# Column 1 of a two-level fast matrix product put into the four-product order, and half of column 3's cast copies replaced by direct loads

## The chip, the cores and the metric

One core of a Trainium2 chip runs the kernel. The metric is the device time of one execution in microseconds (us), as a median of several runs. Engines: PE is TensorE, DVE is VectorE, ACT is ScalarE, POOL is GpSimd and SP is SyncE; POOL and SP also issue DMAs, each into a queue of its own.

## What is computed

```python
def setup_inputs():
    m, k, n = 4096, 4096, 4096
    return {
        "a": np.random.randn(m, k).astype(np.float32),
        "b": np.random.randn(k, n).astype(np.float32),
        "bias": np.random.randn(n).astype(np.float32),
    }

def reference(a, b, bias):
    return np.tanh(np.matmul(a, b) + bias)
```

## The kernel before

**Columns and items.** The output is made in four columns of 1024 (numbered 0 to 3 here, so the "second" is column 1 and the "fourth" column 3). Inside a column the unit of work is an item: two blocks of 128 rows, with all of K. Items are numbered n = 0, 1, 2, ... through the whole program: column 0 has 0 to 12, column 1 has 13 to 28, column 2 has 29 to 44, column 3 has 45 to 60. Data are fp16 with fp32 sums in PSUM.

**One level.** An item's a is cut into four transposed quarters a11, a12, a21, a22 and the column's b into b11, b12, b21, b22. Seven products m1 to m7 of sums of these replace eight (`PRODUCTS`, L36): m2 = s2 b11, m5 = s5 b22, m3 = a11 d3, m1 = s1 d1, m4 = a22 d4, m6 = s6 e6, m7 = s7 e7. A whole product is 16 matmuls of 128x512 (`product`, L466). Seven slots (`SLOTS`, L45) make an item; m6 and m7 of an item are run in the slots of the next, and in between DVE reads the PSUM banks and writes them (`after`, L506).

**Two levels.** Where two items that follow each other are taken together, the same product of both (2 x 16 matmuls of 128x512) can be made as seven half products of 8 matmuls of 128x256 each, 56 in all. The left operands then need sums of two items' quarters (made by DVE into tiles `h`), the right operands sums of quarters of b ("forms"). There are two writings of it. `twice` (L663) is used in column 1 only: m3 for the pairs of items (15,16), (17,18), (19,20), (21,22), m4 for the last three of them, m6 for (17,18) and (19,20), whose forms POOL reads back from DRAM one after the other (`pull`, L799). `twice_four` and `four` (L939, L998) are the **four-product order** of columns 2 and 3: a first pair of items has m3 and m4 at two levels while the forms of m2 and m6 are made by DVE and put into DRAM (`put_four`, L761, and `put_sum`, L780, at the slots in `STAGED`, `ASIDE` and `ADDED`); from the next item on `four` runs two items at a time with m2 to m7 without m1 at two levels. m2's and m6's forms are read back by POOL into five buffers (`pull_four`, L828), the others stay in SBUF. The last two items of column 2 have m6 and m7 as whole products ("leaving", `leave` in `four`), while what was overwritten in b is brought back (`BACK`, L95, `give_back`, L986, at steps numbered in `four`).

**Where a comes from.** Items of column 0, and items 24 to 28 of column 1, are "natural": POOL loads fp32 rows of a with a cast to fp16 (`load_nat`, L234) and DVE transposes them (`turn`, L286); SP keeps the quarters and the first sums in DRAM (`keep`). All other items fetch these by SP (`fetch`, L311). Item 23 is the last of column 1 that fetches.

**Where b comes from.** POOL loads a quarter block of fp32 b with a cast (`load_b`, L369, four DMAs a block). For column 3 all 16 blocks are cast during column 1 from DRAM to DRAM (`cast_b`, L365, at the slots in `CAST`, L91), and are read later by one DMA each. Column 3's blocks 0 and 1 are read when column 2 ends, blocks 2 and 3 an item later (`change`).

**Queues.** SP's and POOL's DMAs wait in the order of the program, each for its data, its buffer and for the landing of the DMA eight places ahead in its own queue (the program has eight DMA semaphores a queue and uses them in turn). A DVE instruction waits at the head of DVE's own line in the same way.

Of the kernel before, what the change touches and what calls it, by code (L numbers as in the profile page):

```python
# [59 lines left out]
TWICE = {1: ("m3", "m4"), 2: ("m3", "m4"), 3: ("m3", "m4")}  # L60
# [26 lines left out]
FOURS = {2: 2, 3: 2}  # L87
# [3 lines left out]
CAST = {3: (-106, -103, -100, -97, -94, -91, -88, -85, -82, -79, -76, -73, -70, -67, -64, -61)}  # L91

# [9 lines left out]
PLACE = {  # L102
# [3 lines left out]
}  # L106
OVER = {"e6": (0, 1), "e7": (1, 0)}
# [16 lines left out]
def kernel(  # L124
# [61 lines left out]
    partner, twos, streams, begins, ends_with, firsts = {}, {}, {}, {}, {}, {}  # L186
    for c in TWICE:
        alone = [
            n for n, item in enumerate(items)
            if item[0] == c and item[2] is None and (c > 1 or item[1][0] in early)  # L190
        ]
        alone = alone[: len(alone) // 2 * 2]
        if c in FOURS:
            firsts[alone[0]] = c
            begins[c], ends_with[c] = alone[FOURS[c]], alone[-1] + 1
            alone = alone[: FOURS[c]]
        partner.update(zip(alone[::2], alone[1::2]))
        twos.update({n: [i for i in TWICE[c] if i == "m3" or n > alone[1] or c in FOURS] for n in alone})
        if c in STREAMED:
            streams[c] = alone[2:-2:2]  # L200
            for n in streams[c]:
                twos[n].append("m6")
                twos[n + 1].append("m6")
    second = {v: k for k, v in partner.items()}
    fours = {n for c in FOURS for n in range(begins[c], ends_with[c])}

    plain = max(n for n in partner if items[n][0] == 1) + 2
    guests = {(plain, "a12"), (plain, "a21")}
# [3 lines left out]

    def by_two(n, what):
        return what in twos.get(n, ())
# [96 lines left out]
    def fetch(n, name):  # L311
        for here, there in stored(n, name):
            nc.sync.dma_start(out=here, in_=there)
# [4 lines left out]
    def new_sum(shape, dt, name, n=None):  # L318
        pool = sums
        if n is None or not (by_two(n, "m6") or by_two(n - 2, "m6") or n in fours or items[n][0] in FOURS and (not again(n) or items[n][2] in SPARED) and n < beginning(n)):  # L320
            turns[0] += 1
            pool = spare if turns[0] % 3 == 0 else sums
# [5 lines left out]
    def asum(n, name, half=None):  # L328
# [8 lines left out]
        elif name == "s6" and n in partner and by_two(n, "m6"):  # L337
            s[name] = side[:, :, ds(NB, NB)].rearrange("p a (b m) -> p a b m", m=P)
# [167 lines left out]
    def after(n, s, what, st):  # L506
# [3 lines left out]
        if what == "m2":  # L510
# [3 lines left out]
            if by_two(n, "m4") and n not in firsts:  # L514
# [6 lines left out]
        elif what == "m5":  # L521
            st["c"] = bank(n, s, "c")
            if by_two(n, "m3"):
# [19 lines left out]
        elif what == "m1":  # L543
            if last:
                st["v"] = bank(n, s, "v")
                if n in partner:
                    (twice_four if c in FOURS else twice)(n, "m3", 2)
# [23 lines left out]
        else:  # L571
            if last:
                if n in twos and n + 2 < len(items) and not again(n + 2) and not natural(n + 2) and n + 2 != plain:
                    fetch(n + 2, "a12")
                o = st["ds"] if n + 2 == plain else new_out()
# [46 lines left out]
    def twice_right(what, name):  # L622
        x, y, op = {
            "d1": ((0, 0), (1, 1), SUB), "d4": ((0, 0), (1, 0), ADD), "d3": ((0, 1), (1, 1), ADD),
            "e6": ((0, 0), (0, 1), ADD), "e7": ((1, 0), (1, 1), ADD),
        }[name]
        over = OVER.get(name)
        for i in range(2):
            if (what, name) in rights:
                to = rights[what, name][:, ds(i * TB, TB)]  # L630
            else:
                to = quarter(what, *over, i)
            tt(to, quarter(what, *x, i), quarter(what, *y, i), op)

    def move(what, c, out_, *names):

        for name, (r, j) in (OVER_FOUR if c in FOURS else OVER).items():
# [9 lines left out]
    def twice_left(n, what, name):  # L647
        left = TWO[what][0]
        which = {
            "s2": ((1, 0), (1, 1)), "s5": ((0, 1), (0, 0)), "s1": ((1, 1), (0, 0)),  # L650
            "s6": ((1, 0), (0, 0)), "s7": ((0, 1), (1, 1)),
        }[name]
        x, y = (
            by_four(aset[(n, partner[n])[i]][left])[:, ds(h * TP // TB, TP // TB)] for i, h in which
        )
        tt(by_four(lefts[PLACE[what][name]]), x, y, SUB)

    def twice_clear(n, what):
# [1236 lines left out]
```

## Time and profile before

| what | value |
|---|---|
| time, median of 3 runs (range) | 1516.98 us (1516.84 to 1517.39) |
| the profiled execution: its time, its span | 1514.7 us, 1513.0 us |
| matmuls of 128x512, of 128x256 in the program | 4773, 4312 |
| DMA, mean over the span | 258 GB/s |
| first two-level matmul of columns 1, 2 and 3 | at 458.7, 838.4 and 1204.0 us of the span |

A page of the profile gives each engine's busy time, the span in 40 slices, the DMA queues, the chain that ended last, and groups of like instructions. Other views of the same trace give the waits of an engine, instructions in order of time, and busy times in chosen windows. PEld is the weight load that goes ahead of each matmul.

### The profile page before, as it was taken

The numbers are of one execution on the slowest core, as the hardware profiler recorded it, in microseconds if no ns is written. First come the engines' busy times: TensorE is split into PE (matmuls) and PEld (weight loads), VectorE is DVE, ScalarE is ACT, GpSimd is POOL, SyncE is SP. The second block draws the span as 40 slices with busy tenths as digits, with TensorE's granted clock in tenths as the row PEclk, the third lists the DMA queues.
The fourth block names the chain that finished last, engine by engine and source line by source line (L and its number), as shares of the span: only waits on it lengthen the run. The fifth ranks groups of instructions, "written<-read, shape, count | busy, mean of one in ns | idle before, by whom it ended". The sixth has DMA issues, their size and how long they took to land.

```text
span 1513.0 us, 24012 instructions
## 1 busy us (share of the span) xinstructions
PE 1505.8 (100%) x9101; PEld 889.8 (59%) x9101; DVE 1182.5 (78%) x1644; ACT 380.3 (25%) x830; POOL 488.9 (32%) x881
## 2 busy tenths in 40 slices
PE   9999999999999999999999999999999999999999
PEld 4444444444445566544444578888744458888887
DVE  6789877777876666577788788889758879888888
ACT  4431111111221122111122223332212222333332
POOL 8775433433603231343453311111112121111112
PEclk9999999999999999999999999999999999999999
DMA  9999999999979998999997978898896687888895
GB/s 186 183 211 259 272 247 214 216 213 243 182 225 283 267 280 267 223 259 243 231 188 239 306 263 300 325 340 301 282 337 205 205 280 268 305 303 315 322 343 188
DMA packets 211255, 390.38 MB, mean 258 GB/s; under 512 B 25538, under 2 KB 107970, under 8 KB 211140
## 3 DMA queue, kind: packets, MB, share of 16 engines
q0 software_dynamic: 118400, 199.02, 57.1%
q1 hardware_dynamic: 92068, 189.44, 36.0%
q8 instruction: 71, 1.16, 0.3%
q10 hardware_dynamic: 672, 0.39, 0.1%
q14 instruction: 44, 0.36, 0.1%
HBM read 337.65 MB, written 136.84 MB: 314 GB/s over the span
## 4 chain that ended last, share of the span: by engine, by line
PE 96%; DMA 2%; DVE 1%; issue 0%; SPq 0%; ACT 0%; DVEq 0%
PE ps L479 55%; PE ps L898 27%; PE ps L1524 5%; PE ps L962 5%; PE ps L679 4%; DMA out_dram<-o 1%; DMA out_dram<-s 0%; DMA a<-scratch 0%; DMA coarse<-in_a_dram 0%; DVE ps L154 0%; PE warm L1584 0%; DVE h L154 0%; PE spread L442 0%; DVE s L154 0%; DVE d L154 0%
## 5 line engine op out<-in xcount | busy, mean ns | idle before, releaser
L479 PEld LDWEIGHTS <-a 128*128 128x128 f16 x3136 | 306.8, 98 | 365.7 <-issue 1.2
L479 PE MATMUL ps<-b,a 128*128 128x512 f16 x1092 | 249.4, 379 | 0.9 <-DVE s L154 0.9
L898 PEld LDWEIGHTS <-h 128*128 128x128 f16 x2176 | 212.7, 98 | 26.9 <-issue 0.5
L834 POOL DMA_DIRECT2D form<-form_m x147 | 77.8, 529 | 411.6 <-PE ps L898 369.1
L479 PE MATMUL ps<-d,a 128*128 128x512 f16 x896 | 202.5, 379 | 0.0
L479 PE MATMUL ps<-e,a 128*128 128x512 f16 x876 | 199.3, 379 | 0.0
L279 DVE STREAM_TRANSPOSE a<-nat 128x1024 f16<-128x1024 f16 (+2 forms) x202 | 175.2, 911 | 19.1 <-PE ps L479 17.6
L898 PEld LDWEIGHTS <-a 128*128 128x128 f16 x1632 | 159.7, 98 | 25.1 <-issue 0.7
L479 PE MATMUL ps<-d,s 128*128 128x512 f16 x624 | 141.0, 379 | 0.0
L251 POOL DMA_DIRECT2D nat<-in_a_dram x176 | 92.9, 533 | 134.2 <-DVE a L279 63.7
L479 PEld LDWEIGHTS <-s 128*128 128x128 f16 x816 | 79.9, 98 | 94.1
L382 POOL DMA_DIRECT2D b<-in_b_dram x192 | 103.4, 545 | 84.2 <-DVE a L279 31.0
L154 DVE TENSOR_TENSOR a<-a,a 128x2048 f16<-128x2048 f16 (+1 forms) x103 | 123.9, 1203 | 0.2
L898 PE MATMUL ps<-form,h 128*128 128x256 f16 x848 | 108.1, 273 | 0.0
L154 DVE TENSOR_TENSOR h<-a,h 128x1024 f16<-128x1024 f16 x136 | 92.6, 687 | 12.3 <-PE ps L898 12.1
L503 ACT ACTIVATE o<-ps 128x512 f32<-128x512 f32 x88 | 52.9, 601 | 152.9 <-issue 97.6
L898 PE MATMUL ps<-form,a 128*128 128x256 f16 x672 | 83.6, 273 | 0.1
L962 PE MATMUL ps<-d,a 128*128 128x512 f16 x352 | 79.4, 379 | 0.0
L154 DVE TENSOR_TENSOR ds<-ds,ps 128x512 f32<-128x512 f32 (+1 forms) x101 | 66.9, 673 | 10.8 <-PE ps L962 5.3
L984 ACT CAST ps<-zeros 128x256 f32<-128x256 f16 x140 | 50.1, 380 | 96.7 <-DVE s L154 51.4
L154 DVE TENSOR_TENSOR ps<-ps,x 128x256 f32<-128x256 f32 x88 | 37.9, 430 | 41.5 <-PE ps L898 26.6
L479 PE MATMUL ps<-side,a 128*128 128x512 f16 x272 | 69.8, 379 | 0.0
(195 smaller groups left out, 1929.5 us busy)
## 6 DMA issues: line engine op xcount, KB each, us to landing
form<-form_m POOLq DMA_DIRECT2D x147, 512.0 KB, 7.1
a<-scratch SPq DMA_DIRECT2D x140, 512.0 KB, 7.2
out_dram<-o SPq DMA_DIRECT2D x199, 256.0 KB, 5.8
nat<-in_a_dram POOLq DMA_DIRECT2D x288, 128.0 KB, 6.5
scratch<-a SPq DMA_DIRECT2D x48, 512.0 KB, 6.7
b<-in_b_dram POOLq DMA_DIRECT2D x160, 128.0 KB, 5.4
scratch<-a SPq DMA_DIRECT2D x32, 256.0 KB, 6.4
cast<-in_b_dram POOLq DMA_DIRECT2D x64, 128.0 KB, 9.7
```

What stands on the lines that cost most here:

```text
L154: nc.vector.tensor_tensor(out=out_, in0=in0, in1=in1, op=op)
L251: nc.gpsimd.dma_start(out=tl[ds(q * QP, QP), :, :], in_=src.rearrange("(mb p) k -> p mb k", p=QP),)
L279: nc.vector.transpose(dst[:, ds(b0 * tb, n * tb), :].rearrange("P (b t) (mb p) -> P mb b t p", t=tb, p=QP), src[:, :, ds(b0, n), :].rearra ...
L382: nc.gpsimd.dma_start(out=dst[ds(q * QP, QP), ds(t, nt)], in_=src)
L479: nc.tensor.matmul(st[where], at, bt, start=(what == "m2" or n < LEAD and what == "m1") and i == 0, stop=i == len(ts_) - 1, skip_group_che ...
L503: nc.scalar.activation(o, src, TANH)
L679: nc.tensor.matmul(to, at, bt, start=False, stop=t == TP - 1, skip_group_check=True)
L834: nc.gpsimd.dma_start(out=rights[what, name], in_=forms[what, name])
L898: nc.tensor.matmul(to, at, bt, start=False, stop=t == TP - 1, skip_group_check=True)
L962: nc.tensor.matmul(to[:, half], at[:, t // TB, t % TB], bop[right, t // TB][:, t % TB, half], start=anew and t == 0, stop=t == T - 1, skip ...
L984: nc.scalar.copy(bank(n, 0, where)[:, HALF[half]], zeros)
L1524: nc.tensor.matmul(mb[m % 4, j], aq[m, kt // T][:, kt % T, :], right(kt, j), start=fresh and kt == k0, stop=stop and kt == k1 - 1, skip_gr ...
```

## The change

Column 1 is run as column 2 is: items 15 and 16 have m3 and m4 at two levels, items 17 and 18, 19 and 20 six of the seven products, and items 21 and 22, which leave, m3, m4, m2 and m5. `twice`, its streamed forms and their tables go. Since natural items follow column 1's last group, its leaving differs from column 2's: `BACK` has a table of its own, with the loads of item 24 ("nat") and item 23's a21 and a12 ("guest") in it; item 23's a11 goes through POOL's queue; the result of m6 is copied to an output tile by ACT; the last m7 (item 22's) is cut into halves that run between item 23's products. Item 24's transposes come a slot later. Of column 3's 16 cast copies eight are left, five at the start of column 1 and three inside column 2's first group; its blocks 2 and 3 are loaded directly.

```diff
-TWICE = {1: ("m3", "m4"), 2: ("m3", "m4"), 3: ("m3", "m4")}
+TWICE = (1, 2, 3)
...
-STREAMED = (1,)
-STREAM = ((1, 1), (0, 0), "d3", "d4", "d1", "e7", "e6")
...
 ADDED = {
+    1: {("m2", "t3"): (-5, -2), ("m6", "t3"): (2, 5)},
...
-STAGED = {2: (-8, -6, -4, 1, 4, 7), 3: (-8, -6, -4, 1, 4, 7)}
-ASIDE = {2: (-7, -5, -3, 1, 3, 6), 3: (-12, -7, -10, -2, 6, 4)}
-SAVED = {2: (-3, -2, 0, 2)}
+STAGED = {1: (-8, -6, -4, 1, 4, 7), 2: (-8, -6, -4, 1, 4, 7), 3: (-8, -6, -4, 1, 4, 7)}
+ASIDE = {1: (-7, -5, -3, 1, 3, 6), 2: (-7, -5, -3, 1, 3, 6), 3: (-12, -7, -10, -2, 6, 4)}
+SAVED = {1: (-3, -2, 0, 2), 2: (-3, -2, 0, 2)}
...
-FOURS = {2: 2, 3: 2}
+FOURS = {1: 2, 2: 2, 3: 2}
...
-CAST = {3: (-106, -103, -100, -97, -94, -91, -88, -85, -82, -79, -76, -73, -70, -67, -64, -61)}
+CAST = {3: (-106, -103, -100, -97, -94)}
+CASTING = {2: (1, 6, 10)}
...
 BACK = {
+    1: {
+        ("e6", 0): 6, ("e6", 1): 7, ("m7", "t3"): 7, ("guest", "a21"): 8, ("b11", 0): 9, ("b11", 1): 9, ("b11", 2): 10,
+        ("b11", 3): 10, ("m5", "t3"): 9, ("m3", "t3"): 14, ("m4", "t3"): 15, ("nat", 1): 11, ("nat", 0): 11,
+        ("guest", "a12"): 10,
+    },
...
-            if later:
+            if leave and natural(m + 1):
+                result(st[i]["s"], pair[i], 1, c, 1)
+            elif later:
                 left_over.append(lambda: end("s", i, 1, 1))
...
             if not last:
-                fetch(m, "a11")
+                fetch(m, "a11", nc.gpsimd if natural(m + 1) else nc.sync)
...
                 take_m6(i)
+                if i == q and natural(m + 1):
+                    at_slot(SLOTS * m + 1, one_whole, "m7", q, range(TP))
+                    at_slot(SLOTS * m + 3, one_whole, "m7", q, range(TP, T))
+                    at_slot(SLOTS * m + 3, take_m7, q)
+                    break
                 one_whole("m7", i)
...
+            if n - 2 in fours:
+                turns = [(i, (x + 1, y + 1)) for i, (x, y) in turns]
```

What stands where is shown at three places. In the names of a row, `ps_7_254` is PSUM bank 7, `x4` counts equal rows, and the numbers behind a name are only its buffer.

**Start of column 1, POOL's queue** (items 13 to 16; `b21` is the last load of column 1's b, `cast_3_...` a cast copy for column 3, `form_m2_k` the DRAM copy of m2's form k, `stage` the SBUF tile it is put from). Before:

```order
L382 DMA b21_3375<-in_b_dram 32x4x512 x4
L382 DMA cast_3_0_0_1_3504<-in_b_dram 128x512 x4
L382 DMA cast_3_1_0_1_3585<-in_b_dram 128x1x512 x4
L382 DMA cast_3_2_0_1_3673<-in_b_dram 128x1x512 x4
L747 DMA form_1_0_3758<-e6_2_3449 128x4x256
```

With the change:

```order
L370 DMA b21_3378<-in_b_dram 32x4x512 x4
L659 DMA form_m2_1_3504<-stage_3505 128x2048
L370 DMA cast_3_0_0_1_3509<-in_b_dram 128x512 x4
L646 DMA form_m2_0_3538<-side_108 128x4x256
L646 DMA form_m2_0_3538<-b11_1_2989 128x4x256
L659 DMA form_m2_3_3569<-stage_3570 128x2048
L666 DMA form_m2_4_3598<-side_108 128x4x256
L666 DMA form_m2_4_3598<-b11_1_2989 128x4x256
L646 DMA form_m2_2_3601<-b11_2_3166 128x4x256
L646 DMA form_m2_2_3601<-b11_3_3171 128x4x256
L370 DMA cast_3_0_1_0_3604<-in_b_dram 128x1x512 x4
L659 DMA form_m2_6_3637<-stage_3638 128x2048
```

Three casts stood free right behind the loads of b; now each stands behind a put that waits for DVE to make its stage tile.

**End of column 1, POOL's queue** (`form_...` a pull of a form, `e6_k` the blocks of e6 brought back, `nat` item 24's rows of a). Before:

```order
L806 DMA form_4980<-form_1_6_3951 128x2048
L823 DMA side_108<-block_1_e6_0_3980 128x4x512
L823 DMA e6_1_5069<-block_1_e6_1_3982 128x2048
L823 DMA e6_2_5071<-block_1_e6_2_3984 128x2048
L823 DMA e6_3_5073<-block_1_e6_3_3986 128x2048
L251 DMA nat_5245<-in_a_dram 32x2x1024 x4
```

With the change:

```order
L694 DMA form_5485<-form_m2_6_3637 128x2048
L683 DMA side_108<-form_m6_0_3798 128x4x256
L683 DMA side_108<-corner_e6_0_3768 128x4x256
L683 DMA e6_1_5521<-form_m6_0_3798 128x4x256
L683 DMA e6_1_5521<-corner_e6_1_3836 128x4x256
L683 DMA e6_2_5602<-form_m6_2_3878 128x4x256
L683 DMA e6_2_5602<-form_m6_5_3989 128x4x256
L683 DMA e6_3_5630<-form_m6_2_3878 128x4x256
L683 DMA e6_3_5630<-form_m6_5_3989 128x4x256
L299 DMA a11_5689<-scratch_5_97 128x2048
L237 DMA nat_5691<-in_a_dram 32x2x1024 x4
L237 DMA nat_5696<-in_a_dram 32x2x1024 x4
```

Item 24's loads now stand behind item 23's a11, whose buffer is free only when m1 of item 21 has run.

**End of column 1, DVE** (`ps_7_254` holds item 23's m2 and then m5, `ps_2_249` takes what m3 adds to). Before, around the first transposes of item 24:

```order
L154 TENSOR_TENSOR ps_5_252<-cs_5368,ps_4_251 128x512
L154 TENSOR_TENSOR a12_5140<-s1_5349,a12_5140 128x2048
L279 STREAM_TRANSPOSE a22_5425<-nat_5245 128x2x16x32
L279 STREAM_TRANSPOSE a22_5425<-nat_5250 128x2x16x32
L154 TENSOR_TENSOR ps_0_247<-ps_7_254,bias_bc_109 128x512
L154 TENSOR_TENSOR s_5460<-ps_7_254,bias_bc_109 128x512
```

With the change:

```order
L152 TENSOR_TENSOR s_5501<-s_5501,ps_1_248 128x512
L152 TENSOR_TENSOR ps_0_247<-ps_7_254,bias_bc_109 128x512
L152 TENSOR_TENSOR s_5818<-ps_7_254,bias_bc_109 128x512
L265 STREAM_TRANSPOSE a22_5820<-nat_5691 128x2x16x32
L265 STREAM_TRANSPOSE a22_5820<-nat_5696 128x2x16x32
L152 TENSOR_TENSOR s1_5832<-a22_5548,a11_5689 128x2048
L152 TENSOR_TENSOR ps_2_249<-ps_7_254,s_5818 128x512
```

The transposes have moved from ahead of the two reads of m2's bank to behind them, and now stand ahead of the instruction that item 23's m3 waits for.

More of the change, by code (lines that the diff above doesn't have):

```diff
@@ L738, in twice_after @@
             result(st["ds"], pair, 1, c, 0)
[L740 to L752 removed]
+    forms, queue = {}, []
     staged = {}
@@ L788, in put_sum @@
             )
-    def put_block(c, name, blk):
-        blocks[c, name, blk] = dram.tile([P, TB, NB], fp16, name=f"block_{c}_{name}_{blk}")
-        nc.gpsimd.dma_start(out=blocks[c, name, blk], in_=bop[name, blk])
-    def begin(c):
-        queue.extend((c, name) for n in streams[c] for name in STREAM)
-        for i in range(4):
-            pull()
-    def pull():
-        if queue:
-            c, name = queue.pop(0)
-            pulled[0] += 1
-            i = pulled[0] % 4
-            pool, tag = (bops, f"e6_{i}") if i else (spare, "sum")
-            rights["m6", name] = pool.tile([P, TP, NB // 2], fp16, name="form", tag=tag)
-            nc.gpsimd.dma_start(out=rights["m6", name], in_=forms[c, name])
     corners = {}
@@ L1784 @@
         at_slot(s0 + 14, new_lefts)
         if c < NC - 1:
-            s1 = SLOTS * max(n for n in partner if items[n][0] == c)
-            for what, there, back in (("m3", 6, 13 if c == 1 else 6), ("m4", 10, 14)):
+            for what, there in (("m3", 6), ("m4", 10)):
                 at_slot(s0 + there, move, what, c, True)
-                if c not in FOURS:
-                    at_slot(s1 + back, move, what, c, False)
     for c in FOURS:
         begin_four(c)
+    casts = []
     for c, slots in CAST.items():
```

296 lines of the change are left out of this document (70 added, 226 removed), and 10 rows, old and new, of tables (BACK, PLACE).

## The prediction

> **What bounds the kernel now.** I read the page first, then PE's waits, the chain that ended last, PE's groups, and windows and the timeline of the stages that the change copies or moves.
>
> ```profile
> PE 1505.8 (100%) x9101; PEld 889.8 (59%) x9101; DVE 1182.5 (78%) x1644; ACT 380.3 (25%) x830; POOL 488.9 (32%) x881
> PEclk9999999999999999999999999999999999999999
> ```
> ```profile
> PE warm L1584 <- DVE idle L417: 1.3, 1, 1.3
> PE ps L479 <- DVE s L154: 0.9, 1, 0.9
> PE tp L1625 <- DVE first L1620: 0.5, 1, 0.5
> PE ps L962 <- DVE s L154: 0.4, 1, 0.4
> PE ps L898 <- DVE ps L154: 0.3, 1, 0.3
> ```
>
> PE is busy for all but 7.2 of 1513.0 us at an undiminished clock, and behind the opening it waits three times, 1.6 us together. So the time is the sum of the matmuls, and a change is worth the matmuls it removes less the waits it makes. Busy can hide slow matmuls, so the chain gives the real spacing (start, length, how many):
>
> ```profile
> 624.25 210.67 PE ps L479 x976
> ...
> 959.23 34.97 PE ps L898 x320
> ```
> ```profile
> L898 PEld LDWEIGHTS <-h 128*128 128x128 f16 x2176 | 212.7, 98 | 26.9 <-issue 0.5
> ```
>
> One 128x512 matmul takes 210.67/976 = 215.9 ns, one 128x256 takes 34.97/320 = 109.3 ns. The half matmul costs 0.506 of the whole; its weight load, 98 ns, fits under it.
>
> **Matmuls.** A product of two items is 32 x 215.9 = 6.91 us whole (3.45 us an item) and 56 x 109.3 = 6.12 us at two levels: 0.79 us saved each. Column 1 has 4 (m3) + 3 (m4) + 2 (m6) = 9 of them before. After: m3 and m4 for the first pair, six for each of two groups, four for the leaving group, 2 + 12 + 4 = 18. So 9 x 32 = 288 matmuls of 512 go and 9 x 56 = 504 of 256 come, which is also the difference of the two programs: 62.2 - 55.1 = **7.1 us saved**, certain as long as nothing waits. There are 216 weight loads more. **A rule against this:** the Trainium skill, "TensorE: Matmul & The Clock Gate", section "Back-to-back issue gap", says that in a real stream of load and matmul pairs the spacing is set by both, and gives 131 ns at N=512 and 81 ns at N=128. An estimate from that page for N=256, on the line between, is 98 ns; the sum would be 49.4 - 37.7 = 11.7 us slower. The rows here are 215.9 and 109.3, so I go by these.
>
> **The stage that is copied.** DVE's instructions from column 1's first sums of b to the middle of its leaving group are now, name for name, those of column 2. So column 2's windows (PE, PEld, DVE, ACT, POOL busy; clock; DMA share) price the new stage:
>
> ```profile
> 576.00:600.00 24.00, 24.00 (x156) 15.10 (x155) 14.29 (x22) 6.31 (x13) 3.96 (x7) 1.00 0.86 282
> ...
> 840.00:864.00 24.00, 23.72 (x152) 14.58 (x151) 19.39 (x30) 5.03 (x12) 9.66 (x13) 1.00 1.06 344
> ...
> 936.00:960.00 24.00, 24.00 (x191) 18.46 (x189) 23.10 (x36) 6.40 (x16) 4.76 (x9) 1.00 0.80 271
> ...
> 1080.00:1104.00 24.00, 23.56 (x117) 11.23 (x115) 11.29 (x17) 5.43 (x10) 0.00 (x0) 1.00 0.99 305
> 1104.00:1128.00 24.00, 23.08 (x108) 10.27 (x107) 10.82 (x14) 4.25 (x8) 3.43 (x6) 1.00 1.05 370
> ```
>
> DVE goes from 14.3 to up to 23.1 of 24 us, and PE still does not wait in the middle (24.00). The waits are at the two ends: 0.28 us at the start, 0.44 + 0.92 us when the column is left. With nothing else I book their sum, **1.6 us**. ACT, at most 9 of 24 us, has room.
>
> **The start, with casts in it.** Timeline of column 2's start:
>
> ```profile
> 833.02 0.70 DVE L154 TENSOR_TENSOR ps<-ps,bias_bc 128x512 f32<-128x512 f32 x1 [3.67 <-ACT o L503]
> ...
> 845.41 0.69 DVE L154 TENSOR_TENSOR o<-ds,ps 128x512 f32<-128x512 f32 x1 [1.02 <-DMA out_dram<-o]
> ...
> 850.11 1.03 PE L898 MATMUL ps<-d,h 128*128 128x256 f16 x8 [0.28 <-DVE ps L154]
> ```
>
> An output store lands late while the DMA engines are full (share 1.06), DVE stands 3.67 and 1.02 us, and PE 0.28 us. Column 1 adds five casts to this. What one takes of the DMA engines comes from the window 395 to 430 us, in which POOL's queue had mostly casts and loads of b (packets, MB, share):
>
> ```profile
> q0 software_dynamic: 4282, 4.65, 77.5%
> ```
> ```profile
> out_dram<-o SPq DMA_DIRECT2D x6, 256.0 KB, 9.7
> ```
>
> The second row is SP's output stores from 818 to 843 us (median to landing). The first is 77.5% of 35 us for 4.65 MB, 5.8 us a MB, 2.9 us for a cast of 0.5 MB. Two of the five fall where column 2's window was half empty; three, 8.7 us, fall into the full one. All of that lies in POOL's queue, and the stores that DVE waits for are in SP's, where 9.7 us to landing is already seen with POOL's queue busy. Bounds: 0 and half of 8.7, 4.4 us; I take 0, the row with both queues busy being the nearest, and keep 4.4. The three casts in column 2's first group stand behind the pulls of forms: one pull issued behind a cast has the least cover:
>
> ```profile
> 899.19 0.53 POOL L834 DMA_DIRECT2D form<-form_m  x1 [2.96 <-PE ps L898]
> ...
> 910.04 1.04 PE L898 MATMUL ps<-form,a 128*128 128x256 f16 x8
> ```
>
> 10.85 us against 7.1 (median to landing, the row below) + 2.9: hidden, by 0.85; at worst 1 us.
>
> **The end of column 1** is where the copy stops being one. Column 2's end:
>
> ```profile
> 1090.91 0.69 DVE L154 TENSOR_TENSOR o<-s,ps 128x512 f32<-128x512 f32 x1 [4.17 <-DMA out_dram<-o]
> ...
> 1092.25 3.61 PE L962 MATMUL ps<-e,a 128*128 128x512 f16 x16 [0.44 <-DVE s L154]
> ...
> 1108.12 0.69 DVE L154 TENSOR_TENSOR s<-ps,bias_bc 128x512 f32<-128x512 f32 x1 [1.16 <-DMA out_dram<-s]
> ...
> 1108.87 1.89 PE L479 MATMUL ps<-b,a 128*128 128x512 f16 x8 [0.92 <-DVE s L154]
> ```
>
> The 0.44 has its cause in the store of an output tile and stays. The 0.92 came because tile s was free only when stored; column 1 copies it away by ACT first, and half of m7 (1.73 us) covers DVE's two reads (2 x 0.7), so that wait goes. What is late next is item 24. Its loads stand on POOL behind item 23's a11, which is free when m1 of item 21 ends (call it 0), and the program gives a queue eight DMAs in flight, so the eighth load waits for a11 to land:
>
> ```profile
> form<-form_m POOLq DMA_DIRECT2D x147, 512.0 KB, 7.1
> a<-scratch SPq DMA_DIRECT2D x140, 512.0 KB, 7.2
> ```
> ```profile
> DMA to landing us min/median/max: 3.0/7.4/12.9
> ```
> ```profile
> 636.38 2.36 DVE L279 STREAM_TRANSPOSE a<-nat 128x1024 f16<-128x1024 f16 x2
> ```
>
> a11 lands at 0.5 + 7.2 = 7.7, the eighth load (third row: item 24's kind) at 15.1. DVE wants it when four whole products (13.8), m2 (3.45), two reads (1.4) and the first transpose (1.18) are done: 19.9. Cover 4.8 us at the medians. At 12.9 for both it is 26.3, 6.4 late, less about 1 us that DVE has left before m3: 5.4 us of waiting. Behind the blocked transposes stand s1 and the instruction that releases m3's bank, so DVE's wait becomes PE's. Bounds 0 and 5.4; I keep the 0.92 that disappears as its allowance.
>
> SP's queue moves too: the last of b11's blocks is issued behind m5's output store, some 11 us before item 23's m2 reads it. That covers
>
> ```profile
> b<-form_m SPq DMA_DIRECT2D x5, 256.0 KB, 5.6
> ```
>
> and even the 9.7 us of a store; cost 0.
>
> **Column 3's loads.** Eight reads become 32 loads on POOL, in front of m2's form puts. The first of the blocks concerned was read at
>
> ```profile
> 1124.04 0.53 POOL L372 DMA_DIRECT2D b<-cast  x1 [12.46 <-PE ps L479]
> ```
> ```profile
> 1152.00:1164.00 12.00, 12.00 (x58) 5.45 (x56) 10.64 (x12) 3.00 (x5) 0.00 (x0) 1.00 0.27 98
> ```
> ```profile
> DVE d L154 <- DMA b<-in_b_dram: 2.4, 3, 1.2
> ```
>
> 32 loads at 0.73 us of DMA time each (2.9/4) end near 1148, and the DMA engines stand at 0.27 soon after; the first sum that needs them is nine slots of 3.45 us, 31 us, behind this row. So that lull hides them: cost 0. If the cover is gone, DVE waits as the third row has it for loads of this kind in the columns before, 2.4 us in three waits; I keep 2.4 as the upper end.
>
> **The sum** against the profiled execution: 1514.7 - 7.1 + 1.6 = 1509.2. The median shown is 2.3 us above that execution, so the same difference, -5.5, gives **1511.5 us**.
>
> **Rivals.** (1) Item 24 late once or at both halves, by 3 to 5.4 us: 1514.5 to 1516.9. For it, the DMA share of 0.99 and 1.05 in the end of column 2; against, 4.8 us of cover. (2) Casts extend the store's landing by 4.4 us: 1515.9; the share of 1.06 speaks for it, the separate queue against. (3) **Slower:** the loads of items 24 and 25 never catch up. Each of their four halves is loaded into buffers which the one before must free, and all stand in one queue; two halves late by 5.4 us make 10.8: 1522.3. It decides once all waits exceed 7.1 + 3.0 us. For it, every DVE wait there is handed on to PE; against, the row
>
> ```profile
> 642.56 4.20 POOL L251 DMA_DIRECT2D nat<-in_a_dram  x8 [6.69 <-DVE a L279]
> ```
>
> shows POOL idle for 6.69 us before eight of these loads: it waits for buffers and not for bandwidth, and can make up for lost time. (4) Weight loads not hidden: 216 x 98 ns = 21.2 us more, 1532.7; the spacing of 109.3 speaks against it. The Trainium skill's page named above would have it so; its 131 and 81 ns give an estimate of 1516.98 + 11.7 = 1528.7. That the matmuls are not saved is ruled out by the count.
>
> **Chances.** Forecast 0.71, rival 1 0.13, rival 2 0.06, rival 3 0.09, rival 4 0.01. The forecast's own range is 1509.6 (no wait at all is 1516.98 - 7.1 = 1509.9, and the runs shown scatter by up to 0.4) to 1514; up to 1516.0, with most of rival 1 and rival 2, some 0.86 is held, and what is left out lies above. A measurement tells 0.2%, 3.0 us, from no change: faster is below 1514.0 (forecast and 0.02 of rival 1: 0.73), slower above 1520.0 (rivals 3 and 4: 0.10), the same between them (the rest of rivals 1 and 2: 0.17).
>
> **What would show it.** PE busy lower by about 7 us; L898's successor with 1.5 times the matmuls in column 1's stretch and 109 ns each; PE's waits as a list of four or five of under 1 us. Right at the start: a DVE wait for an output store, as at 845, and a PE wait of 0.3. At column 1's end: DVE's first transposes with no DMA named ahead of them. Wrong: a PE wait of some us released by DVE there, with "DMA nat" behind it; PE waiting for a form in column 2's first group; or "DMA b" ahead of a sum in column 3.

## The result, and the profile after the change

Slower: 1534.76 us (median; 1533.04 to 1535.62) against 1516.99 us, a ratio of 1.0115 (95% interval 1.0098 to 1.0133). The forecast was 1511.5 us, the range 1509.6 to 1516.0. The profiled execution's span is 1533.9 us against 1513.0, 20.9 us more. The page after the change, engines and granted clock:

```profile
PE 1508.1 (98%) x9317; PEld 913.6 (60%) x9317; DVE 1214.0 (79%) x1702; ACT 395.9 (26%) x883; POOL 518.2 (34%) x916
PEclk9999999999999999899999999999999999999999
```

PE's busy time grew by 2.3 us although 7.1 us of matmuls went, and its share fell from 100% to 98%. One slice has an 8 for the clock. PE's waits after the change (line, releaser: us in total, times, longest):

```profile
PE ps L822 <- DVE s L152: 10.2, 2, 9.7
PE ps L467 <- DVE s L152: 3.5, 1, 3.5
PE ps L467 <- DMA b<-form_m: 2.7, 3, 1.1
PE ps L758 <- DMA form<-form_m: 2.0, 1, 2.0
...
PE ps L758 <- DVE ps L152: 0.8, 1, 0.8
...
PE ps L758 <- ACT ps L775: 0.2, 1, 0.2
```

Together 19.4 us behind the opening, where 1.6 were before. Of these 17.4 stand at three places: 3.5 at column 1's start (457 to 461 us), 9.7 and 2.2 at its end (632 to 656), 2.0 in column 2's first group (939 to 941). In each of them or right behind it the clock is down. Windows of the run after (PE, PEld, DVE, ACT and POOL busy; clock; DMA share; GB/s):

```profile
460.00:480.00 20.00, 19.02 (x111) 11.18 (x111) 17.83 (x30) 5.79 (x14) 8.44 (x13) 0.91 1.09 318
...
640.00:650.00 10.00, 7.94 (x30) 3.32 (x30) 3.17 (x5) 1.89 (x3) 5.86 (x11) 0.74 1.13 229
650.00:660.00 10.00, 7.78 (x29) 2.88 (x28) 3.07 (x5) 0.63 (x1) 0.02 (x1) 0.83 1.03 303
...
940.00:950.00 10.00, 8.65 (x64) 7.14 (x65) 5.94 (x10) 3.53 (x9) 1.06 (x2) 0.83 1.02 414
```

A clock of 0.91 over 20 us is 3.6 us at half speed, 1.8 us lost; the others lose 1.7 each, and 1.5 in 640 to 650, where PE worked only from 642.06. That is 6.7 us. The sum: -7.1 (matmuls) + 17.8 (waits, 19.4 - 1.6) + 6.7 (clock) = 17.4. Another 2.2 us came about at the very opening, which the change does not touch: by 12 us PE had run 39 matmuls, 49 before. The first ones of 128x512 stand 427 ns apart, twice the later 215.9, and that lasts until about 10.3 us after and 5.7 us before; the 4.6 us between are 2.3 us lost. (2.6 to 4.2 us were lost up to 440 us in the runs below, which all have this opening, so this scatters by itself.) That makes 19.6 of 20.9.

**The largest wait, column 1's end.** Timeline of the run after, SP's stores, then DVE and PE:

```profile
625.87 4.49 SPq L482 DMA_DIRECT2D out_dram<-o  x3
...
640.72 0.69 DVE L152 TENSOR_TENSOR o<-s,ps 128x512 f32<-128x512 f32 x1 [13.29 <-DMA out_dram<-o]
...
642.06 5.12 PE L822 MATMUL ps<-e,a 128*128 128x512 f16 x16 [9.72 <-DVE s L152]
```

The output tiles `o` are a ring of three; DVE wants a fourth and stands until the first is stored, 14.8 us after its issue. PE's next bank is released by DVE's instruction behind that one. Column 2's end, in the same run, has the same instructions:

```profile
1105.15 2.59 SPq L482 DMA_DIRECT2D out_dram<-o  x3
...
1111.53 0.69 DVE L152 TENSOR_TENSOR o<-s,ps 128x512 f32<-128x512 f32 x1 [4.24 <-DMA out_dram<-o]
```

There the store lands in 6.4 us, DVE waits 4.24, PE 0.5. So up to about 4 us of DVE's wait were covered, and all beyond went to PE one for one. SP's own order differs: in column 1 block 1 of b11 and the move back of m5's form are issued ahead of the three stores, in column 2 behind them (e4 below takes that up). The company differs too. DMA queues of the run after, first 1104 to 1112 us (column 2's end), then 642 to 650 (packets, MB, share of the 16 engines):

```profile
q1 hardware_dynamic: 3242, 2.57, 108.0%
...
q0 software_dynamic: 9, 0.02, 0.7%
```
```profile
q0 software_dynamic: 787, 1.29, 87.6%
q1 hardware_dynamic: 1010, 0.51, 24.2%
```

q1 is SP's queue, q0 POOL's. Alone, SP's moved 2.57 MB in 8 us, with some 800 bytes to a packet, since stores were among them; beside POOL's loads of item 24 it moved 0.51 MB, with some 500 bytes to a packet against 1.6 KB in POOL's. How long the blocks of b11 and the stores took to land, issued in 615 to 652 us (count, size, median):

```profile
b<-form_m SPq DMA_DIRECT2D x5, 256.0 KB, 19.0
out_dram<-o SPq DMA_DIRECT2D x4, 256.0 KB, 13.9
```

The prediction had reckoned with 5.6 us for the first and 0.44 us of PE's time for the second.

**Column 1's start** has the same chain with ACT in DVE's place. DMA in 430 to 470 us, before and after:

```profile
q0 software_dynamic: 1193, 2.27, 23.2%
...
out_dram<-o SPq DMA_DIRECT2D x8, 256.0 KB, 2.2
```
```profile
q0 software_dynamic: 3665, 6.17, 59.2%
...
out_dram<-o SPq DMA_DIRECT2D x6, 256.0 KB, 12.5
```
```profile
458.88 0.60 ACT L491 ACTIVATE o<-ps 128x512 f32<-128x512 f32 x1 [7.81 <-DMA out_dram<-o]
```

Puts and casts made what POOL's queue moves 2.7 times as much, a store's landing went from 2.2 to 12.5 us (median), ACT stood 7.81 us for a free output tile, DVE for ACT, and PE 3.5 us for DVE. **In column 2's first group** a pull stands right behind a cast in POOL's queue:

```profile
923.67 2.21 POOL L370 DMA_DIRECT2D cast<-in_b_dram  x4
928.35 0.56 POOL L694 DMA_DIRECT2D form<-form_m  x1 [2.47 <-PE ps L758]
...
941.35 2.91 PE L758 MATMUL ps<-form,a 128*128 128x256 f16 x16 [1.99 <-DMA form<-form_m]
```

### The profile page after: what moved, and what is told of

Read it like the earlier page. It is cut to its first block, busy times and chain, and to the rows that moved or that the text cites. A ratio compares the mean times of both kernels' runs of the same rounds, so it can differ in the third digit from the quotient of the medians.

```text
span 1533.9 us, 24646 instructions
## 1 busy us (share of the span) xinstructions
PE 1508.1 (98%) x9317; PEld 913.6 (60%) x9317; DVE 1214.0 (79%) x1702; ACT 395.9 (26%) x883; POOL 518.2 (34%) x916
## 4 chain that ended last, share of the span: by engine, by line
PE 90%; DMA 7%; DVE 1%; issue 1%; ACT 0%; SPq 0%; POOL 0%; DVEq 0%; ACTq 0%; POOLq 0%
PE ps L467 45%; PE ps L758 32%; PE ps L822 6%; PE ps L1398 5%; DMA out_dram<-o 3%; DMA b<-form_m 1%; DMA a<-scratch 1%; DMA form<-form_m 1%; DMA nat<-in_a_dram 1%; DMA coarse<-in_a_dram 0%; SPq L683 0%; DVE h L152 0%; DVE o L152 0%; DVE form L152 0%; PE warm L1458 0%
## 5 line engine op out<-in xcount | busy, mean ns | idle before, releaser
L467 PEld LDWEIGHTS <-a 128*128 128x128 f16 x2784 | 272.7, 98 | 334.6 <-issue 7.3
L758 PEld LDWEIGHTS <-h 128*128 128x128 f16 x2752 | 269.6, 98 | 35.3 <-issue 1.2
L694 POOL DMA_DIRECT2D form<-form_m x182 | 96.7, 532 | 511.1 <-PE ps L758 455.7
L758 PEld LDWEIGHTS <-a 128*128 128x128 f16 x2064 | 202.3, 98 | 34.6 <-DMA form<-form_m 2.3
L467 PE MATMUL ps<-b,a 128*128 128x512 f16 x924 | 214.0, 382 | 6.2 <-DVE s L152 3.5
L467 PE MATMUL ps<-e,a 128*128 128x512 f16 x756 | 172.0, 379 | 0.0
L152 DVE TENSOR_TENSOR a<-a,a 128x2048 f16<-128x2048 f16 (+1 forms) x121 | 145.8, 1205 | 0.2
L758 PE MATMUL ps<-form,h 128*128 128x256 f16 x1056 | 134.6, 273 | 0.0
L152 DVE TENSOR_TENSOR h<-a,h 128x1024 f16<-128x1024 f16 x172 | 117.0, 687 | 15.7 <-PE ps L758 15.6
L467 PE MATMUL ps<-d,s 128*128 128x512 f16 x528 | 119.3, 379 | 0.0
L758 PE MATMUL ps<-form,a 128*128 128x256 f16 x832 | 104.6, 274 | 2.1 <-DMA form<-form_m 2.0
L822 PEld LDWEIGHTS <-a 128*128 128x128 f16 x576 | 57.0, 99 | 74.9 <-issue 14.3
```

Of the source, the lines that this page charges most:

```text
L152: nc.vector.tensor_tensor(out=out_, in0=in0, in1=in1, op=op)
L467: nc.tensor.matmul(st[where], at, bt, start=(what == "m2" or n < LEAD and what == "m1") and i == 0, stop=i == len(ts_) - 1, skip_group_che ...
L694: nc.gpsimd.dma_start(out=rights[what, name], in_=forms[what, name])
L758: nc.tensor.matmul(to, at, bt, start=False, stop=t == TP - 1, skip_group_check=True)
L822: nc.tensor.matmul(to[:, half], at[:, t // TB, t % TB], bop[right, t // TB][:, t % TB, half], start=anew and t == 0, stop=t == T - 1, skip ...
```

## The experiments

**The theory:** both queues share the 16 DMA engines and take turns packet by packet; beside POOL's packets of 2 to 4 KB SP's of 512 bytes (blocks of b11, and moves, which bring back from DRAM what the forms had overwritten) crawl, the stores behind them land late, and the ring of three hands that to PE. **Rivals:** SP's own order (the blocks of b11 ahead of the stores); and capacity (more to move at column 1's end than the engines can, in any order).

The table gives the time that PE lost, worked out from the start of every matmul in each trace: what the next one starts later than 215.9 ns (128x512) or 109.2 ns (128x256) behind it, where that is over 0.1 us; waits and half clock alike. The columns are stretches of the span in us. Each run's time stands beside the kernel before on the same chip (one run each; medians in the row "after" and from e12 on). The four times of the changed kernel spread over 2.6 us, so between single runs the stretches tell more than the times. The traces of e12, e13 and e14 are of executions of 1519.0, 1518.2 and 1518.8 us, slower than their medians.

| run | 440-500: start of column 1 | 500-612 | 612-675: its end | 675-1080: column 2 | 1080-1160: into column 3 | time, before |
|---|---|---|---|---|---|---|
| before | 0.0 | 0.0 | 0.0 | 0.8 | 1.7 | |
| after | 5.6 | 0.6 | 15.4 | 4.6 | 1.3 | 1534.8, 1517.0 |
| e1 no casts | 1.1 | 0.2 | 14.6 | 0.2 | 10.1 | 1533.3, 1516.8 |
| e2 own tile for o | 6.6 | 0.2 | 12.6 | 5.4 | 1.5 | 1533.4, 1516.8 |
| e3 quarter of the loads | 5.3 | 0.4 | 16.4 | 2.8 | 2.6 | 1534.0, 1516.8 |
| e4 SP's order | 6.2 | 0.5 | 20.7 | 2.3 | 1.6 | 1538.0, 1516.8 |
| e5 b11 by POOL | 5.3 | 0.7 | 9.6 | 2.4 | 2.3 | 1526.3, 1515.5 |
| e6 gated loads | 5.1 | 0.8 | 7.7 | 3.0 | 2.0 | 1524.9, 1515.5 |
| e7 quiet casts | 0.9 | 1.9 | 13.8 | 1.7 | 1.5 | 1526.2, 1515.5 |
| e8 e5 and e7 | 1.0 | 1.9 | 7.2 | 2.9 | 1.8 | 1521.8, 1515.5 |
| e9 moves by POOL | 0.8 | 1.5 | 11.7 | 1.0 | 1.7 | 1522.6, 1516.7 |
| e10 casts at the turn | 0.7 | 0.2 | 10.7 | 2.9 | 1.8 | 1522.5, 1516.7 |
| e11 before, 8 casts | 0.0 | 0.0 | 0.0 | 1.0 | 2.6 | 1517.3, 1516.7 |
| e12 by due time | 1.0 | 0.2 | 2.9 | 5.4 | 2.8 | 1515.1, 1516.2 |
| e13 two at each turn | 0.9 | 0.5 | 4.3 | 2.6 | 2.3 | 1514.9, 1516.4 |
| e14 six casts | 0.8 | 0.5 | 2.8 | 2.1 | 6.4 | 1517.6, 1516.4 |

**e1, no casts.**
```diff
-CAST = {3: (-106, -103, -100, -97, -94)}
-CASTING = {2: (1, 6, 10)}
+CAST = {}
+CASTING = {}
```


> The changed kernel without its eight cast copies: all 16 blocks of b of column 3 are loaded directly. Theory (the loss is made by transfers that share the 16 DMA engines packet by packet, at three places): the 3.5 us wait at column 1's start (458 to 461 us) and the 2.0 us wait inside column 2's first group (939 to 941 us) go, with the half-clock stretch of 3.4 us behind each; the wait of 9.7 us where column 1 leaves stays. 1534.8 less 5.6 and 3.8 is 1525, plus 0 to 5 us for column 3's loads. Rival (the form puts alone fill the engines at column 1's start, casts or not): 1531 to 1535, and PE still waits some 3 us at 458.

Measured 1533.3, which is the rival's range, but not for the rival's reason. At the two places the theory holds: 5.6 us became 1.1, column 2's 4.6 became 0.2. So the puts alone are not enough at the start; it takes the casts beside them. But column 3's start paid 10.1 us, 8.8 more than with the casts and not at most 5, so the casts earn their place.

**e2, a tile of its own for the fourth output.**
```diff
-            st[i]["o"] = new_out()
+            if leave and natural(m + 1) and i == q:
+                st[i]["o"] = wide.tile([P, 2, NB], fp32, name="o", tag="wide")[:, 0]
+            else:
+                st[i]["o"] = new_out()
```


> The changed kernel, where the sum of item 22's m5 goes to a tile of its own instead of the fourth use of the ring of three output tiles; nothing else. Theory (DVE stood 13.3 us for the landing of a store, since the ring of three was full, and PE 9.7 us behind it): DVE's wait at 627 us goes and PE's 9.7 us with it, and the half clock behind it (1.5 us): 1534.8 less 11.2 is 1523.5; the waits for blocks of b11 (2.2 us) stay or grow by 2 to 4 us. Rival (PE is held in that stretch by b11's blocks or by DVE's own work as much as by the ring): PE waits 6 us or more for blocks of b11 instead, 1529 to 1532.

Measured 1533.4, somewhat over the rival's range. PE's waits of e2:

```profile
PE ps L467 <- DMA b<-form_m: 9.7, 1, 9.7
```

DVE's wait for the store is gone, and PE stands as long for b11 a little later. The ring is only where the lateness shows first; everything in SP's queue is late.

**e3, a quarter of item 24's loads.**
```diff
+            elif c == 1 and n == ends_with[1] + 1 and (r, u) != (1, 0):
+                tl = nat[n, 1, 0]
             elif part is None:
```


> The changed kernel with 4 of item 24's 16 loads of a; its four quarters are transposed from the one tile that is loaded, so item 24's products are of other data. Theory (item 24's loads in POOL's queue take turns with SP's 512-byte packets on the same engines and so hold SP's stores up): the store that landed after 14.8 us lands after 6 to 8 us, DVE's wait for it falls from 13.3 us to 4 to 6 us, PE's of 9.7 us to under 2 us: 1534.8 less 11 to 14 is 1521 to 1524. Rival (SP's own queue is the cause: blocks of b11 and moves stand ahead of the stores in it): the store still takes 12 us or more and the time stays at 1531 to 1535.

Measured 1534.0: it tells nothing, for the load was not less. Loads issued in 615 to 652 us, after and e3:

```profile
nat<-in_a_dram POOLq DMA_DIRECT2D x24, 128.0 KB, 6.7
```
```profile
nat<-in_a_dram POOLq DMA_DIRECT2D x24, 128.0 KB, 6.5
```

POOL's queue was free sooner and went straight on to item 25's loads. e6 asks the same by delay.

**e4, SP's order as at column 2's end.**
```diff
-        ("e6", 0): 6, ("e6", 1): 7, ("m7", "t3"): 7, ("guest", "a21"): 8, ("b11", 0): 9, ("b11", 1): 9, ("b11", 2): 10,
-        ("b11", 3): 10, ("m5", "t3"): 9, ("m3", "t3"): 14, ("m4", "t3"): 15, ("nat", 1): 11, ("nat", 0): 11,
+        ("e6", 0): 6, ("e6", 1): 7, ("m7", "t3"): 7, ("guest", "a21"): 8, ("b11", 0): 9, ("b11", 1): 10, ("b11", 2): 16,
+        ("b11", 3): 16, ("m5", "t3"): 11, ("m3", "t3"): 14, ("m4", "t3"): 15, ("nat", 1): 11, ("nat", 0): 11,
```


> The changed kernel with SP's order at column 1's end as it is at column 2's: b11's block 1 one step later, m5's move back two steps later, b11's blocks 2 and 3 behind the stores of m2's sums and m5's (step 16). Theory (both queues share the engines; fewer small packets stand ahead of the stores): the store lands after some 9 us instead of 14.8, PE's wait falls from 9.7 to 3 to 5 us, but b11's blocks 2 and 3 come 3 to 6 us later to item 23's m2: 1526 to 1532. Rival (SP's order alone is the cause): the store lands within 6 to 7 us, PE waits under 1 us there as in column 2, 1519 to 1523.

Measured 1538.0, above both ranges. DVE's wait for the store fell from 13.29 to 2.8 us, but b11's last blocks then stood behind d's moves:

```profile
DVE o L152 <- DMA out_dram<-o: 2.8, 1, 2.8
```
```profile
PE ps L467 <- DMA b<-form_m: 19.1, 2, 18.3
```

So SP's order decides which transfer is late, and column 2's order does not mend column 1's end: 20.7 us are lost there. An order of SP's with b11 behind the stores but ahead of d's moves was not run, so SP's order is not ruled out as part of the cause.

**e5 and e6: b11 by POOL; item 24's loads delayed.**
```diff
-                    bring_block(name, part, nc.gpsimd if step < DIRECT else nc.sync)
+                    bring_block(name, part, nc.gpsimd if step < DIRECT or c == 1 else nc.sync)
```
```diff
-        ("b11", 3): 10, ("m5", "t3"): 9, ("m3", "t3"): 14, ("m4", "t3"): 15, ("nat", 1): 11, ("nat", 0): 11,
+        ("b11", 3): 10, ("m5", "t3"): 9, ("m3", "t3"): 14, ("m4", "t3"): 15, ("nat", 1): 13, ("nat", 0): 13,
...
                 take_m6(i)
+                if i == p and natural(m + 1):
+                    gate = dram.tile([P, 1], fp32, name="gate")
+                    nc.gpsimd.dma_start(out=gate, in_=st[p]["s"][:, ds(0, 1)])
+                    give_back(c, 13)
```


> The changed kernel with b11's four blocks brought back through POOL's queue, ahead of item 23's a11 and item 24's loads, instead of SP's. Theory (SP's 512-byte packets take turns with POOL's packets of 2 KB and more on the same engines, so SP's queue crawls while POOL's is full): SP then has 2 MB less in that stretch, the store that landed after 14.8 us lands within 8, b11 comes with POOL's large packets, and PE loses 1 to 3 us at column 1's end instead of 15.5: 1520 to 1523. Rival (there is simply more to move in 610 to 650 us than the engines move, whichever queue has it): the wait goes over to item 23's a11 or item 24's loads, still 8 us or more lost, 1528 to 1535.

> The changed kernel with item 24's loads held in POOL's queue behind a copy of 512 bytes that reads item 21's sum after m6, so that they begin some 8 us later and nothing else moves. Theory: SP's queue has the engines alone until then, the store lands within 7 us, b11's blocks within 10, PE's waits of 9.7 and 2.2 us fall under 1 each, and item 24's loads still land ahead of its transposes or cost up to 4 us there: 1520 to 1525. Rival (too much to move in that stretch in any order): the same 15 us appear as a wait for item 24's transposes, 1530 to 1535.

Measured 1526.3 and 1524.9: the end of column 1 falls from 15.4 to 9.6 and 7.7 us, about half of it each time: e5 between theory and capacity, e6 within the theory's range. Timeline of e5, then of e6:

```profile
636.90 0.69 DVE L152 TENSOR_TENSOR o<-s,ps 128x512 f32<-128x512 f32 x1 [11.35 <-DMA out_dram<-o]
```
```profile
631.93 0.69 DVE L152 TENSOR_TENSOR o<-s,ps 128x512 f32<-128x512 f32 x1 [6.66 <-DMA out_dram<-o]
...
652.09 1.25 DVE L265 STREAM_TRANSPOSE a<-nat 128x1024 f16<-128x1024 f16 x1 [2.72 <-DMA nat<-in_a_dram]
```

In e5 b11 comes in time, but the store, still in SP's queue, waits 11.35 us beside b11's packets in POOL's. In e6 hardly anything but the loads' start differs, and DVE's wait falls from 13.29 to 6.66, PE's from 9.72 to 2.93: the loads in POOL's queue do hold SP's stores up. Part comes back as a wait for the loads themselves. DMA queues of e6 in 626 to 634 us:

```profile
q1 hardware_dynamic: 3126, 2.14, 89.5%
q0 software_dynamic: 182, 0.62, 21.2%
```

Here POOL's queue is nearly out of the way and SP's fills the engines itself, so much of the 6.66 us that are left is SP's own traffic ahead of the store.

**e7 and e8: casts at quiet steps; both mended.**
```diff
-CAST = {3: (-106, -103, -100, -97, -94)}
-CASTING = {2: (1, 6, 10)}
+CAST = {3: ()}
+CASTING = {17: (1,), 19: (1, 5), 21: (1,), 33: (1,), 35: (1, 5), 37: (1,)}
...
-            if first and k in CASTING.get(c, ()):
+            if k in CASTING.get(n, ()):
```


> The changed kernel with the eight cast copies moved: none at column 1's start, one at step 1 of each group of four of columns 1 and 2 (items 17, 19, 21, 33, 35, 37), one more at step 5 of items 19 and 35, where POOL's next pull of a form is some 10 us away. Theory: the loss of 5.6 us at column 1's start and of 3.8 us in column 2's first group go, column 1's end keeps its 15.5: 1534.8 less 9 is 1526. Rival (a cast of 1 MB read costs 3 us of all engines wherever it stands): pulls or SP's fetches come late elsewhere, 1530 to 1535.

> Both of the two kernels before: b11 by POOL, and the eight casts at the quiet steps. Theory: 1534.8 less 9 and less 12 to 14 is 1511 to 1514, faster than the kernel before the change. Rival (capacity): 1522 or more.

e7 measured 1526.2, as the theory said: 5.6 became 0.9, column 2's 4.6 became 1.7, at 1.3 us more in column 1's groups. e8 measured 1521.8, the rival's figure: 7.2 us are left at column 1's end, the largest wait in them (3.2 us) now for d's moves. Its DMA queues in 642 to 648 us:

```profile
q0 software_dynamic: 607, 1.00, 88.6%
q1 hardware_dynamic: 608, 0.33, 24.4%
```

607 packets against 608, as turns packet by packet would have it, and with 1.65 KB to a packet against 0.54 POOL's gets three times the bytes. The counts are not equal everywhere: in the changed kernel's own 642 to 650 us, above, they are 787 and 1010.

**e9 and e10: the four moves by POOL too; casts at the turns.**
```diff
-                    move(name, c, False, part)
+                    move(name, c, False, part, queue=nc.gpsimd if c == 1 else nc.sync)
...
-        ("b11", 3): 10, ("m5", "t3"): 9, ("m3", "t3"): 14, ("m4", "t3"): 15, ("nat", 1): 11, ("nat", 0): 11,
+        ("b11", 3): 10, ("m5", "t3"): 9, ("m3", "t3"): 7, ("m4", "t3"): 7, ("nat", 1): 11, ("nat", 0): 11,
```
```diff
-CASTING = {17: (1,), 19: (1, 5), 21: (1,), 33: (1,), 35: (1, 5), 37: (1,)}
+CASTING = {17: (1,), 33: (1,), 35: (1, 5), 37: (1,)}
...
         fetch(m + 1, "a21")
+        for i in range({1: 1, 2: 2}.get(c, 0)):
+            casts.pop(0)()
         free.extend(("e6_2", "e6_3"))
```


> The kernel with b11 by POOL and quiet casts, and the four moves back at column 1's end (m7's, m5's, m3's, m4's form t3) also in POOL's queue, m3's and m4's two at step 7 already. In the kernel before it PE lost 5.7 us at 650 to 658, waiting for d<-away_m_t and scratch<-a of SP's queue, whose packets of 512 bytes go one for one with POOL's of 2 KB. Theory (turns packet by packet): nothing of 512 bytes is left in SP's queue there, those 5.7 us fall under 1.5, item 24's loads begin 2 to 4 us later and cost at most 2 us: 1521.8 less 2 to 4.5 is 1517 to 1520. Rival (capacity): the 5 us come back as waits for a11 or item 24's loads, 1521 to 1524.

> The same, with three of column 1's and column 2's casts moved to where POOL waits some 20 us at the turn into the groups of four (one in column 1, two in column 2, ahead of the pulls into e6's buffers) and none left in column 1's later groups. Theory (a cast costs only what it takes from transfers under way; the engines are under half busy there): some 2 us lost at 540 to 610 go, 1515 to 1518. Rival: the pulls right behind the moved casts come late, a wait for a form of 2 us or more at 510 or 900: 1518 to 1522.

Measured 1522.6 and 1522.5, both outside what the theory said. The wait for d's moves went, and a new one came (e9):

```profile
PE ps L822 <- DMA e<-form_m: 8.7, 2, 7.9
```

e6's last block is needed first and stood behind half of b11 and four moves in POOL's queue. So with nearly everything in one queue its order counts. e10's turn did save column 1's 1.3 us, and column 2 lost 1.9 more. The engines are not under half busy all through those waits of POOL: in e8 their share is 0.98 in 480 to 485 us and 0.31 in 485 to 490.

**e11, the kernel before with half of its casts.**
```diff
-CAST = {3: (-106, -103, -100, -97, -94, -91, -88, -85, -82, -79, -76, -73, -70, -67, -64, -61)}
+CAST = {3: (-106, -103, -100, -97, -94, -91, -88, -85)}
...
-        which = [(blk, h, j) for h, j in ((0, 1), (1, 0), (0, 0), (1, 1)) for blk in range(4)]
+        which = [(blk, h, j) for blk in range(2) for h, j in ((0, 1), (1, 0), (0, 0), (1, 1))]
```


> The kernel before the change with half of its casts: the first eight slots hold column 3's blocks 0 and 1, blocks 2 and 3 are loaded directly; column 1's order stays. Theory (the casts and direct loads cost nothing by themselves, only beside the form traffic that the new order of column 1 brings): within 2 us of the kernel before, so 1515 to 1519. Rival (column 3's direct loads cost what the cast copies saved): 1520 or more, with PE waits at 1100 to 1140.

Measured 1517.3 against 1516.7, as the theory said: by themselves eight casts at column 1's start and eight direct blocks cost nothing that shows.

**e12, all that comes back by POOL, in the order of need.**
```diff
-        ("e6", 0): 6, ("e6", 1): 7, ("m7", "t3"): 7, ("guest", "a21"): 8, ("b11", 0): 9, ("b11", 1): 9, ("b11", 2): 10,
-        ("b11", 3): 10, ("m5", "t3"): 9, ("m3", "t3"): 7, ("m4", "t3"): 7, ("nat", 1): 11, ("nat", 0): 11,
+        ("e6", 0): 6, ("e6", 1): 7, ("m7", "t3"): 7, ("guest", "a21"): 8, ("b11", 0): 10, ("b11", 1): 10, ("b11", 2): 10,
+        ("b11", 3): 10, ("m5", "t3"): 10, ("nat", 1): 11, ("m3", "t3"): 11, ("m4", "t3"): 11, ("nat", 0): 11,
...
-CASTING = {17: (1,), 33: (1,), 35: (1, 5), 37: (1,)}
+CASTING = {17: (1,), 33: (1,), 35: (1,), 37: (1,)}
...
-        for i in range({1: 1, 2: 2}.get(c, 0)):
+        for i in range({1: 1, 2: 3}.get(c, 0)):
```


> All that comes back at column 1's end in POOL's queue, in the order in which PE needs it: e6's blocks, m7's move, b11, m5's move, item 23's a11, half of item 24's loads, m3's and m4's moves, the other half; casts as in the kernel before, but three of column 2's at the turn and none at step 5. In the two kernels before, 9 to 11 us were lost there to e6's last block, which stood behind b11 and two moves in POOL's queue. Theory (some 7 us of the 15.5 lost at column 1's end were order and packets, the rest is more to move there than fits): 3 to 6 us stay lost at 620 to 660, 1515 to 1518. Rival (it is order and packets alone): under 2 us lost there, 1512 to 1514. Second rival (capacity alone): again 8 us or more, 1520 to 1523.

Ratio to before 0.9995 (0.9986 to 1.0005): no difference. PE's waits of e12, column 1's end being the first and 0.7 of the fourth:

```profile
PE ps L467 <- DVE ps L152: 1.8, 1, 1.8
PE ps L758 <- DVE h L152: 1.7, 3, 1.2
PE ps L758 <- ACT ps L775: 1.4, 1, 1.4
PE ps L467 <- DVE s L152: 1.4, 2, 0.7
```

Of the 15.4 us at column 1's end 2.9 are left, and the clock stays at 1.00 there. So most of them were queue and order. What is left, just under what was expected, is mostly the wait of the prediction's rival 1, item 24 late. Timeline of e12, DVE and then PE:

```profile
643.04 1.25 DVE L265 STREAM_TRANSPOSE a<-nat 128x1024 f16<-128x1024 f16 x1 [2.13 <-DMA nat<-in_a_dram]
...
646.06 3.61 PE L467 MATMUL ps<-d,a 128*128 128x512 f16 x16 [1.84 <-DVE ps L152]
```

The DMA engines are full from 612 to 675 us (share 1.06), and the loads now stand behind b11 in POOL's queue; no run tells whether capacity or that order makes them late. Column 2's turn, with its third cast, lost 3.0.

**e13 and e14: two casts at each turn; six casts.**
```diff
-        for i in range({1: 1, 2: 3}.get(c, 0)):
+        for i in range({1: 2, 2: 2}.get(c, 0)):
```
```diff
-CASTING = {17: (1,), 33: (1,), 35: (1,), 37: (1,)}
+CASTING = {33: (1,), 37: (1,)}
```


> The kernel by due time, with two casts at the turn of each of columns 1 and 2 instead of one and three. In the kernel before, PE lost 3.0 us at 880 to 890, where DVE waited 4.2 us for fetches of a and 3.3 us for a store, right behind the three casts of column 2's turn. Theory (a cast takes its 3 us from whatever is under way; two fit into the idle engines of each turn, the third does not): those 3.0 us fall under 1.2, nothing grows at 510: a ratio to the kernel before the change of 0.996 to 0.999. Rival (the casts' place does not matter any more, the loss moves along with them): 0.999 to 1.002, with the loss at 500 to 520.

> The same with six casts: those at step 1 of items 17 and 35 are left out, and two more quarter blocks of column 3 are loaded directly. Theory (each cast that is left out frees 3 us of the engines in columns 1 and 2, each direct load costs as much where column 2 ends, which already waits 1.5 to 2.5 us there): 1 us less in columns 1 and 2, 1.5 to 3 us more at 1090 to 1140: 0 to 2 us over the kernel with eight. Rival (column 3 takes two more direct loads for nothing): 1 us under it.

e13: ratio 0.9988 (0.9979 to 0.9997), the lowest of all, 0.1% under the kernel before, only just beyond the measurement's scatter and not told apart from e12. e14: 1.0006 (0.9997 to 1.0015); columns 1 and 2 save 2.1 us against e13, column 3's start loses 4.1 more, both above what was expected. There e14 has a wait that e13 has not:

```profile
PE ps L467 <- DMA a<-scratch: 3.0, 1, 3.0
```

A cast costs where it crowds others, a direct load costs in column 3, and of the two numbers run in this version, six and eight, eight does better.

## Why the prediction was wrong

- **Matmuls, -7.1 us: right.** 9317 of them run, the two-level spacing stays (192 in 21.12 us of the chain, 110 ns), and -7.1 plus the lost time of the two traces (32.1 us after, 5.3 before, the opening's narrower matmuls included) gives 19.7 of the 20.9 us.
- **The end of column 1: the step that failed.** It priced SP's queue at the landing times of column 2's end, where POOL's queue was empty ("cost 0" for b11's blocks, 5.6 us to landing, and 0.44 us for the store; the 9.7 us that it also held against b11 were a store's), and item 24's loads only by when they land themselves. What these loads do to SP's transfers beside them was no term. Measured: the store landed after 14.8 us, b11 after 19.0 us (median), and PE lost 15.4 us. The row of 4.17 us of DVE's wait and 0.44 of PE's had said how little it takes: PE had no cover left. And in the trace before the DMA engines are already full in this very stretch (share 1.10), with PE not waiting and nothing added yet; the prediction went by column 2's rows instead:

```profile
624.00:648.00 24.00, 24.00 (x114) 10.91 (x112) 16.93 (x22) 3.08 (x5) 10.49 (x20) 1.00 1.10 253
```

- **Item 24 itself (rival 1): hidden, not refuted.** After the change DVE's transposes have no wait for the loads, but they come some 15 us late themselves. In e12, where that lateness is gone, the loads are waited for, and PE loses 1.84 us to it: less than the 3 to 5.4 us of the rival.
- **The start: wrong in its reason.** Rival 2's "separate queue against" took two queues for two roads. The bound of 4.4 us held for the wait alone (3.5), not with the 1.8 us of half clock behind it.
- **Three casts in column 2's first group: mis-sized.** 0, at worst 1, was 2.0 us of wait and 1.7 of clock: the pull landed 13 us after its issue, where 10.0 (7.1 + 2.9) were reckoned.
- **Rival 3 had the sign and not the mechanism:** loads that never catch up, and no such wait occurred. **Column 3's direct loads** cost nothing that shows (1.3 us in that stretch, 1.7 before), as forecast.
- **The clock was no term at all.** A fully busy PE gave no row for it, and the waits cost a third more than they last.

The equal packet counts of e8 are what a page states that the prediction did not draw on: the Trainium skill, "DMA: Bandwidth & Descriptors", section "Queues, rings and completion order", says that each DMA engine goes round the queues that have work for it and changes over at packet boundaries. The trace of e8 agrees (607 and 608), that of the changed kernel only roughly (787 and 1010). The page counts some 9 to 17 descriptors to a packet; what SP's packets carried here is 512 bytes, by size a single row of such a block.

What stays open: a transfer that goes over to POOL's queue gets larger packets and another place in the order at once, and no run changes the packets alone. And some 3 to 4 us at column 1's end were not removed, nor did any version save more than 0.1% over the kernel before.

## What to carry to other kernels

Where DMA engines are near full, price a transfer with what runs beside it at the new place, all queues together: a landing time from a stretch with the other queue empty is no bound. When a wait of some us already reaches the bottleneck by a few tenths, its cover is used up, and every further us counts in full. Inside a queue, put first what is due first. And transfers of short rows did badly here in a queue beside one with long packets; that packet size alone does it was not tested.

## What the hardware showed unexpectedly

- **The shares went by packets:** with both queues full, 607 and 608 packets in 6 us, but 1.00 and 0.33 MB. Alone, SP's queue moved 2.57 MB in 8 us, stores of larger packets among them.
- **Short waits cost clock.** The wait of 2.0 us at 939 was followed by 3.4 us at half clock (0.83 over 10 us). In e6 a wait of 2.6 us was not, row below. The Trainium skill, "TensorE: Matmul & The Clock Gate", section "Part 1: The HAM clock gate", has the activity judged in windows of some 3.4 us that run freely, and the clock drop after at least one idle window. The length agrees; that a whole window must be idle does not, since 2.0 us were enough here. Free windows may be why one wait of 2 us cost clock and a longer one did not, but no run here shows where they begin.

```profile
650.00:660.00 10.00, 7.42 (x35) 3.32 (x34) 7.91 (x11) 0.82 (x2) 5.84 (x11) 1.00 1.12 252
```
